# Prefix logsumexp on one core: where the loads stand in ScalarE's instruction stream

## Chip, cores and metric

The kernel runs on one core of a Trainium2 chip. The metric is the device time of one execution in microseconds; lower is better.

## The reference

For each batch and each column the reference runs down the sequence and keeps a running log of a sum of exponentials:

```
B, S, D = 4, 4096, 4128                       # x is random normal, float32
out[:, 0, :] = x[:, 0, :]
for t in range(1, S):
    mx = np.maximum(out[:, t-1, :], x[:, t, :])
    out[:, t, :] = mx + np.log(np.exp(out[:, t-1, :] - mx) + np.exp(x[:, t, :] - mx))
```

So `out[b, t, d]` is the log of the sum of `exp(x[b, s, d])` over all `s` up to `t`. Input and output are 270.5 MB each.

## The kernel before

The kernel computes Exp of the input, prefix sums, and Ln of the sums, and does not keep a running maximum (a last flag sends unsuitable data to a slow general path, `_general`, which is not taken here).

**Tiles.** A tile ("step" in the code) holds 128 x r consecutive rows of one batch and all 4128 columns; partition p holds r neighbouring rows. r is 3 for most tiles and 2 for seven of them. There are n = 45 tiles, numbered 0 to 44: 11 for each of the first three batches (tiles 0, 16 and 27 have two rows) and 12 for the last one, where tiles 37, 39, 43 and 44 have two. A tile lives in one of four slots in SBUF (`SLOTS = 4`, `x0` to `x3`), tile t in slot t mod 4, and everything is done in place: the load writes the slot, Exp, the sums and Ln rewrite it, the store reads it. So load t + 4 may only start once store t has landed; its instruction waits for that.

**Chunks.** The columns are worked on in three chunks (`NC = 3`) of 1376. For each chunk: ScalarE's `exp` (L125); VectorE's `sums` (L153 and L163), which add a partition's own rows; `head`, matmuls on TensorE with a triangular matrix (L171) that give each partition the sum of all rows above it; VectorE's `add`, which adds that to the rows (L187 and L196 for chunks 0 and 1, L181 for chunk 2); and ScalarE's `log` (L206 and L207 for chunks 0 and 1, a pair of Ln; L202, one Ln, for chunk 2). VectorE's `fold` (L143) carries the last sums of a tile into the next one. `head`, `add` and `log` of a chunk need those before them, and the `add` of a tile needs the `fold` that needs the Exp of chunk 2.

**Queues.** All transfers of the main path are issued from ScalarE's queue: `load` (L104; tiles 1 and 2 row by row, L106) and `store` (L111). ScalarE's sequencer takes its instructions in order. A DMA instruction that must wait holds back every Exp and Ln behind it. A store waits for the three Ln of its tile.

**Order.** Three lists, `act`, `vec` and `pe`, fix the order on ScalarE, VectorE and TensorE. They are written by the loop over t near the end of the function: for each chunk c it appends some Exps of the next tile (`exps`, how many is in `turns` or `usual_turn`), then `log`, `add` and `head` of tile t; after the chunks comes `store` t and, in the kernel before, at once the load of tile t + 3 (for t from 2 on), whose slot was emptied by store t - 1. The usual order on ScalarE is: Ln of chunk 0, two Exps of the next tile, Ln of chunk 1, Exp, Ln of chunk 2, store, load. Two places differ: load 4 comes after the second Exp of tile 3, and load 44 (the last) comes right behind load 43 after store 40, though its slot is the one that store 40 empties. The loads of tiles 0 to 3 stand ahead of everything.

Of the kernel before, what the change touches and what calls it, by code (L numbers as in the profile page):

```python
# [15 lines left out]
SLOTS = 4  # L16
# [8 lines left out]
def kernel(  # L25
# [87 lines left out]
    class Chunk:  # L113
# [36 lines left out]
        def sums(self):  # L150
            r, e, got = self.t.r, self.row, []
            if r == 3:
                got.append(nc.vector.tensor_tensor(out=e[1], in0=e[0], in1=e[1], op=ALU.add))  # L153
                for free in () if self.passed else made.get(("log", self.t.n - 1, self.c), ()):
                    tc.add_manual_dep(
                        got[0].ins, free.ins.name,
                        mybir.DependencyInfo(
                            mybir.DependencyClass.Sync, mybir.DependencyReason.DATA,
                        ),
                        reason="the next sum writes what this Ln reads",  # L160
                    )
            n = P if self.passed else P - 1
            got.append(nc.vector.tensor_tensor(  # L163
                out=self.z[0:n], in0=e[r - 2][0:n], in1=e[r - 1][0:n], op=ALU.add,
            ))
            return got
# [46 lines left out]
    steps = []  # L213
# [11 lines left out]
    n = len(steps)  # L225

    lists = {"act": [], "vec": [], "pe": []}
    act, vec, pe = lists["act"], lists["vec"], lists["pe"]
# [17 lines left out]
    }  # L246
    given = {"exp": [0] * n, "sums": [0] * n}

    due = []

    def exps(t, k):
        while t < n and given["exp"][t] < k:
            act.append(("exp", t, given["exp"][t]))
            given["exp"][t] += 1
            if due and given["exp"][t] == due[0][1]:
                act.append(("load", due.pop(0)[0]))

    def passing(t):
        if t and steps[t - 1].last:
# [4 lines left out]
    def sums(t, k):  # L264
        while t < n and given["sums"][t] < k:
# [3 lines left out]
            if c == PASSED - 1 and t:  # L269
                passing(t)  # L270

    exps(0, 2)
    for t in range(n):
        ahead_exps, ahead_sums = turns.get(t, usual_turn)
        exps(t, NC)
        sums(t, 2)
        for c in range(NC):
            exps(t + 1, ahead_exps[c])
            act.append(("log", t, c))
            sums(t + 1, ahead_sums[c])  # L280
            vec.append(("add", t, c))
            if c == 0:
                sums(t, NC)
            pe.append(("head", t, c))
        act.append(("store", t))
        if t == 1:
            due.append((SLOTS, 2))
        elif t and t + SLOTS - 1 < n - 1:
            act.append(("load", t + SLOTS - 1))
            if t + SLOTS == n - 1:  # L290
                act.append(("load", n - 1))
        exps(t + 1, ahead_exps[NC])
        sums(t + 1, ahead_sums[NC])
    passing(n)
# [151 lines left out]
```

## Time and profile before

| | |
|---|---|
| time, median of 3 runs | 1279.49 us (1278.05 to 1281.15) |
| the profiled execution's own time | 1278.78 us |
| its span, first to last instruction | 1277.0 us |
| VectorE busy | 1047.4 us (82%) |
| ScalarE busy | 929.8 us (73%) |
| TensorE matmul busy | 579.5 us (45%) |
| bytes read and written | 270.53 MB and 270.53 MB, 424 GB/s over the span |

Times in the rows of the profile count from the first instruction of the profiled execution. On engines' names: PE is TensorE, PEld its weight loads, DVE VectorE, ACT ScalarE, and ACTq stands for what ScalarE's sequencer issues, the DMAs here. A row of the timeline has the start, the duration, the engine, the line, the operation and the tiles, and in brackets the idle time before it and what ended that. For a DMA row the duration is that of the issuing instruction (with the wait between two that are merged in one row); the time to landing stands in other views. A row for L125 with x2 merges two Exps.

### The profile page before, as it was taken

The numbers are of one execution on the slowest core, as the hardware profiler recorded it, in microseconds if no ns is written. First come the engines' busy times: TensorE is split into PE (matmuls) and PEld (weight loads), VectorE is DVE, ScalarE is ACT, GpSimd is POOL, SyncE is SP. The second block draws the span as 40 slices with busy tenths as digits, with TensorE's granted clock in tenths as the row PEclk, the third lists the DMA queues.
The fourth block names the chain that finished last, engine by engine and source line by source line (L and its number), as shares of the span: only waits on it lengthen the run. The fifth ranks groups of instructions, "written<-read, shape, count | busy, mean of one in ns | idle before, by whom it ended". The sixth has DMA issues, their size and how long they took to land.

```text
span 1277.0 us, 2720 instructions
## 1 busy us (share of the span) xinstructions
PE 579.5 (45%) x812; PEld 225.4 (18%) x812; DVE 1047.4 (82%) x534; ACT 929.8 (73%) x367; POOL 3.8 (0%) x16
## 2 busy tenths in 40 slices
PE   3454544544454353354544424345445435444163
PEld 1121211211111121122111111112112112112021
DVE  3998978888988697798898858689889868788395
ACT  6977877777767676697677668588767767675594
POOL 1000000000000000000000000000000000000000
PEclk9667656665666686666665657676666666776576
DMA  9999999999999999999999999999999999999968
GB/s 398 429 432 432 430 434 434 430 433 434 433 431 432 435 435 431 434 430 422 430 439 430 435 431 436 432 432 427 419 424 444 424 437 434 440 390 424 395 298 364
DMA packets 13550, 541.24 MB, mean 424 GB/s; under 512 B 1504, under 2 KB 1504, under 8 KB 1504
## 3 DMA queue, kind: packets, MB, share of 16 engines
q10 hardware_dynamic: 13536, 541.07, 98.6%
q8 instruction: 6, 0.10, 0.0%
q14 instruction: 8, 0.07, 0.0%
HBM read 270.53 MB, written 270.53 MB: 424 GB/s over the span
## 4 chain that ended last, share of the span: by engine, by line
DMA 49%; ACT 34%; DVE 15%; ACTq 1%; issue 0%
DMA x<-in_x_dram 36%; ACT x L125 21%; DMA out_dram<-x 13%; ACT x L202 5%; ACT x L206 5%; DVE x L187 5%; DVE z L196 3%; ACT x L207 3%; DVE x L181 2%; DVE x L143 2%; DVE x L163 1%; DVE z L163 1%; DVE x L153 1%; ACTq L111 0%; DVE z L190 0%
## 5 line engine op out<-in xcount | busy, mean ns | idle before, releaser
L171 PE MATMUL p<-z,carried 128*128 128x512 f32 (+1 forms) x492 | 356.1, 888 | 472.8 <-DVE z L163 304.2
L125 ACT ACTIVATE x<-x 128x4128 f32<-128x4128 f32 (+1 forms) x135 | 461.5, 3452 | 125.3 <-DMA x<-in_x_dram 89.3
L206 ACT ACTIVATE x<-x 128x2752 f32<-128x2752 f32 (+1 forms) x90 | 208.0, 2312 | 200.6 <-DVE z L196 165.1
L153 DVE TENSOR_TENSOR x<-x 128x1376 f32<-128x1376 f32 x114 | 180.8, 1586 | 180.2 <-ACT x L125 180.2
L171 PEld LDWEIGHTS p<-z,carried 128*128 128x128 f32 x492 | 138.6, 300 | 691.9 <-DVE z L163 336.3
L171 PE MATMUL p<-x,summed 128*128 128x512 f32 (+1 forms) x270 | 189.8, 865 | 151.2 <-DVE x L163 151.2
L187 DVE TENSOR_TENSOR x<-p,x 128x2752 f32<-128x2752 f32 (+1 forms) x90 | 250.9, 2788 | 1.3 <-PE p L171 0.9
L181 DVE SCALAR_TENSOR_TENSOR x<-p,inner,x 128x4128 f32<-128x4128 f32 (+1 forms) x45 | 193.0, 4288 | 1.3 <-PE p L171 1.2
L163 DVE TENSOR_TENSOR z<-x 127x1376 f32<-127x1376 f32 x90 | 143.2, 1591 | 20.6 <-ACT x L125 18.0
L202 ACT ACTIVATE x<-x 128x4128 f32<-128x4128 f32 (+1 forms) x45 | 155.3, 3450 | 4.0 <-DVE x L181 4.0
L196 DVE TENSOR_TENSOR z<-x 128x1376 f32<-128x1376 f32 x82 | 130.6, 1592 | 2.8
L171 PEld LDWEIGHTS p<-x,summed 128*128 128x128 f32 x270 | 73.3, 289 | 264.6 <-DVE x L163 176.8
L207 ACT ACTIVATE x<-z 128x1376 f32<-128x1376 f32 x90 | 120.0, 1333 | 0.0
L163 DVE TENSOR_TENSOR x<-x 128x1376 f32<-128x1376 f32 x45 | 71.6, 1591 | 1.3
L143 DVE TENSOR_TENSOR x<-p,x 1x1376 f32<-1x1376 f32 x41 | 64.7, 1577 | 8.9 <-ACT x L125 8.9
L171 PE MATMUL p<-z,below 128*128 128x512 f32 (+1 forms) x48 | 33.7, 864 | 55.2 <-DVE z L163 42.1
L171 PEld LDWEIGHTS p<-z,below 128*128 128x128 f32 x48 | 13.3, 297 | 76.3 <-issue 32.1
L135 DVE TENSOR_REDUCE short<-x 1x1 f32<-1x4128 f32 x3 | 13.3, 4430 | 0.0
L190 DVE CUSTOM_DVE_ANT_0 z<-x 128x1376 f32<-128x1376 f32 x8 | 12.7, 1592 | 0.3
L146 DVE TENSOR_REDUCE probe<-p 1x1 f32<-1x1376 f32 x4 | 6.3, 1571 | 0.0
L348 ACT ACT_TABLE_LOAD x1 | 1.3, 1283 | 4.8 <-issue 4.8
L128 ACT ACTIVATE x<-x,twice 1x1376 f32<-1x1376 f32 x3 | 4.3, 1441 | 0.2
(23 smaller groups left out, 6.8 us busy)
## 6 DMA issues: line engine op xcount, KB each, us to landing
out_dram<-x ACTq DMA_DIRECT2D x38, 6192.0 KB, 26.0
x<-in_x_dram ACTq DMA_DIRECT2D x36, 6192.0 KB, 40.2
x<-in_x_dram ACTq DMA_DIRECT2D x7, 4128.0 KB, 31.9
out_dram<-x ACTq DMA_DIRECT2D x7, 4128.0 KB, 24.1
x<-in_x_dram ACTq DMA_DIRECT2D x6, 2064.0 KB, 27.7
```

The lines of the kernel that those rows point to most:

```text
L125: got = [nc.scalar.activation(self.e, self.e, ACT.Exp)]
L135: return [nc.vector.tensor_reduce(out=short[:, self.t.b - 1:self.t.b], in_=self.t.xt[0:1, 0, :], op=ALU.min, axis=AX.X,)]
L143: return [nc.vector.tensor_tensor(out=to, in0=pt[0:1], in1=to, op=ALU.add)]
L153: got.append(nc.vector.tensor_tensor(out=e[1], in0=e[0], in1=e[1], op=ALU.add))
L163: got.append(nc.vector.tensor_tensor(out=self.z[0:n], in0=e[r - 2][0:n], in1=e[r - 1][0:n], op=ALU.add,))
L171: nc.tensor.matmul(self.pt[:, a:b], lhsT=w, rhs=self.z[:, a:b], start=True, stop=True,)
L181: return [nc.vector.scalar_tensor_tensor(out=self.e, in0=base, scalar=inner[:, 0:1], in1=self.e, op0=ALU.mult, op1=ALU.add,)]
L187: got = [nc.vector.tensor_tensor(out=e, in0=base, in1=e, op=ALU.add)]
L196: nc.vector.tensor_tensor(out=self.z, in0=ends[0], in1=ends[1], op=ALU.add)
L202: return [nc.scalar.activation(self.e, self.e, ACT.Ln)]
L206: nc.scalar.activation(e, e, ACT.Ln),
L207: nc.scalar.activation(self.row[r - 1], self.z, ACT.Ln),
```

## The change

The change moves `load` instructions within ScalarE's list and nothing else; the other engines' lists stay as they were. `due` becomes a table from tile number to a count of steps, and a new function `turn` appends a step (an `exp` or a `log`; the Ln pair of one chunk counts as one) and then counts down, appending each load whose count has come to zero.

- After the store of a 3-row tile t (t from 2 on) the load of tile t + 3 comes one step later.
- After the store of a 2-row tile it comes two steps later. For t = 1 it is two steps as well; load 4 then stands behind the first Exp of tile 3 instead of the second.
- Load 44 is given six steps from store 40 on. These are Ln of tile 41 chunk 0, two Exps of tile 42, Ln of chunk 1, an Exp, and Ln of chunk 2: the load stands behind that Ln and ahead of store 41.

```diff
-    due = []
+    due = {}
+
+    def turn(step):
+        act.append(step)
+        for t in sorted(due):
+            due[t] -= 1
+            if due[t] == 0:
+                del due[t]
+                act.append(("load", t))
 
     def exps(t, k):
         while t < n and given["exp"][t] < k:
-            act.append(("exp", t, given["exp"][t]))
+            turn(("exp", t, given["exp"][t]))
             given["exp"][t] += 1
-            if due and given["exp"][t] == due[0][1]:
-                act.append(("load", due.pop(0)[0]))
...
             exps(t + 1, ahead_exps[c])
-            act.append(("log", t, c))
+            turn(("log", t, c))
...
         act.append(("store", t))
-        if t == 1:
-            due.append((SLOTS, 2))
-        elif t and t + SLOTS - 1 < n - 1:
-            act.append(("load", t + SLOTS - 1))
-            if t + SLOTS == n - 1:
-                act.append(("load", n - 1))
+        if t and t + SLOTS - 1 < n - 1:
+            due[t + SLOTS - 1] = 1 if steps[t].r == 3 and t > 1 else 2
+        if t + SLOTS == n - 1:
+            due[n - 1] = 6
         exps(t + 1, ahead_exps[NC])
```

## The prediction

> **What bounds the kernel now.** I read first the page's slices, queues and transfer sizes.
>
> ```profile
> GB/s 398 429 432 432 430 434 434 430 433 434 433 431 432 435 435 431 434 430 422 430 439 430 435 431 436 432 432 427 419 424 444 424 437 434 440 390 424 395 298 364
> q10 hardware_dynamic: 13536, 541.07, 98.6%
> out_dram<-x ACTq DMA_DIRECT2D x38, 6192.0 KB, 26.0
> x<-in_x_dram ACTq DMA_DIRECT2D x7, 4128.0 KB, 31.9
> ```
>
> All traffic is on one queue (q10), whose packets fill 98.6% of the 16 DMA engines' span. Most slices run at 429 to 435 GB/s; the last two at 298 and 364. No engine is near that, so the question is where the queue runs empty. Stretches of time show it (columns: stretch, length, busy time and count of PE, PEld, DVE, ACT, POOL, clock, DMA share, GB/s):
>
> ```profile
> 300.00:400.00 100.00, 44.84 (x59) 16.97 (x58) 84.61 (x43) 72.41 (x27) 0.00 (x0) 0.64 1.00 433
> 896.00:902.00 6.00, 3.88 (x5) 1.80 (x6) 5.93 (x4) 2.71 (x2) 0.00 (x0) 0.61 1.06 380
> 1116.00:1124.00 8.00, 4.54 (x7) 1.92 (x8) 7.97 (x7) 6.32 (x4) 0.00 (x0) 0.79 0.81 347
> 1155.00:1207.00 52.00, 13.48 (x20) 5.66 (x21) 28.43 (x15) 28.98 (x11) 0.00 (x0) 0.62 1.00 432
> 1208.00:1220.00 12.00, 6.77 (x10) 2.48 (x8) 11.93 (x7) 9.33 (x4) 0.00 (x0) 0.57 0.55 234
> 1230.00:1240.00 10.00, 6.55 (x11) 2.50 (x9) 9.97 (x6) 9.57 (x5) 0.00 (x0) 0.74 0.55 238
> 1250.00:1255.00 5.00, 3.66 (x6) 1.45 (x6) 4.97 (x5) 2.61 (x2) 0.00 (x0) 0.73 0.86 370
> 1260.00:1268.00 8.00, 0.19 (x2) 0.09 (x2) 4.09 (x6) 4.17 (x3) 0.00 (x0) 0.66 0.71 305
> ```
>
> Against 433 GB/s the four last stretches miss (433 - 234)/433 x 12 = 5.5 us, 4.5, 0.7 and 2.4, together 13.1 us; 1116:1124 misses 1.6. The rest of the run leaves almost nothing to win. Why the queue runs dry at the end is in the waits (engine, line, what was waited for: total us, times, longest) and in the timeline of ScalarE and VectorE:
>
> ```profile
> ACT x L125 <- DMA out_dram<-x: 33.7, 6, 6.9
> ACT x L206 <- DMA out_dram<-x: 23.0, 1, 23.0
> 1171.81 0.34 ACTq L111 DMA_DIRECT2D out_dram<-x  x1
> 1172.19 22.57 ACTq L104 DMA_DIRECT2D x<-in_x_dram  x2
> 1172.82 1.59 DVE L196 TENSOR_TENSOR z<-x 128x1376 f32<-128x1376 f32 x1
> 1194.80 2.50 ACT L206 ACTIVATE x<-x 128x2752 f32<-128x2752 f32 x1 [23.02 <-DMA out_dram<-x]
> 1198.44 7.16 ACT L125 ACTIVATE x<-x 128x4128 f32<-128x4128 f32 x2
> 1216.33 0.35 ACTq L111 DMA_DIRECT2D out_dram<-x  x1
> 1222.61 4.87 ACT L125 ACTIVATE x<-x 128x2752 f32<-128x2752 f32 x2
> 1237.05 0.35 ACTq L111 DMA_DIRECT2D out_dram<-x  x1
> 1252.09 0.34 ACTq L111 DMA_DIRECT2D out_dram<-x  x1
> 1264.61 0.34 ACTq L111 DMA_DIRECT2D out_dram<-x  x1
> ```
>
> Store 40 goes at 1171.81, loads 43 and 44 right behind. Load 44 refills the slot that store 40 empties, so ScalarE's sequencer stands until that store has landed, at 1194.4. The Ln behind it had its input at 1172.82 + 1.59 = 1174.4. The whole tail chain (Ln 41, Exp 42, Ln 41, store 41, then stores 42, 43, 44) starts 20 us late, and no load is left to hide that.
>
> **The change, the last load first.** Landings of load 44 (issued 1194.41), store 41 (1216.33) and all stores (the smallest is the last one's):
>
> ```profile
> DMA to landing us min/median/max: 19.4/19.4/19.4
> DMA to landing us min/median/max: 16.7/16.7/16.7
> DMA to landing us min/median/max: 11.1/26.0/33.7
> ```
>
> A 3-row tile is 6192 x 1024 B = 6.34 MB, 14.6 us at 433 GB/s; a 2-row tile 4128 KB, 9.7 us. Load 44 landed at 1213.8, which is store 40's 1194.4 plus 9.7 (load 43) plus 9.7: the queue works in order, each landing one transfer after the one before. Into an empty queue store 41 took 16.7 - 14.6 = 2.1 us more, so a transfer keeps the queue full if it is issued 2.1 us before its predecessor lands.
>
> Now load 43 stands behind Ln 41 chunk 0, and load 44 behind six steps, the last of them Ln 41 chunk 2, right ahead of store 41. ScalarE goes on at 1174.4, the Ln pair ends at 1178.1, and Exp 42 meets load 42, which lands 14.6 us before store 40, at 1179.8. From the two Exps' start to store 41 the timeline has 1216.33 - 1198.5 = 17.8 us; so store 41 goes at about 1180.0 + 17.8 = 1197.8. Load 44's wait ends at 1194.4, just when its place comes up (3.5 us before store 41, the last Ln's length); queued behind it is only that store, which waits for the Ln anyway. From store to store the timeline has 20.7, 15.0 and 12.5 us: stores 42, 43, 44 go at 1218.5, 1233.6 and 1246.1. The covers for that: Exp 43 starts 6.3 us behind store 41, at 1204.1, as load 43 lands; Exp 44 comes behind store 42, after 1218.5, load 44 landed at 1213.8. Queue: load 44 1213.8, store 41 1228.4, store 42 1243.0, store 43 1252.7, store 44 1262.4. The issues are needed by 1211.7, 1226.3, 1240.9, 1250.6: margins 13.9, 7.8, 7.3 and 4.5 us, so no pause is left. The end moves from 1264.61 + 11.1 = 1275.7 to 1262.4, 13.3 us; by the stretches above it is 13.1. I take 13.2. VectorE's share in the chain is inside the store-to-store distances.
>
> **Loads one step behind the store, 3-row tiles.** A usual place, by the timeline and the chain of waits (start, duration; a DMA's piece is issue to landing):
>
> ```profile
> 410.31 26.02 DMA out_dram<-x
> 412.95 2.50 ACT L206 ACTIVATE x<-x 128x2752 f32<-128x2752 f32 x1 [2.67 <-DVE z L196]
> 415.36 1.33 ACT L207 ACTIVATE x<-z 128x1376 f32<-128x1376 f32 x1
> 293.35 40.20 DMA x<-in_x_dram
> 333.57 7.18 ACT x L125 x2
> ```
>
> The step is a Ln pair that waits 2.67 us for VectorE, so the load goes between 415.4 and 416.7 instead of 410.7, up to 6 us later. The store ahead of it lands at 436.3: the load still has 20 us in the queue, and its landing, fixed by the transfers ahead, doesn't move. Price nothing; without that cover each load would pay its delay. Behind it on ScalarE stands the next Exp or Ln, which loses 0.4 us of issue time as before. Load 4 comes one Exp earlier instead; if it must wait for store 0, it holds the next Exp by one Exp's length at most (7.18 / 2 = 3.6 us), in a slice (the third) that runs at 432 GB/s. Also nothing.
>
> **Two steps behind a 2-row tile's store.** ScalarE stood on an earlier store at six loads (33.7 us), all near 2-row tiles; it now computes at least one step first. Around five of them the slices show 431 to 437 GB/s, so that gives nothing. The sixth is behind the 2-row tile 37 (its store, load 40, store 38; then landings of load 40 and store 38):
>
> ```profile
> 1082.25 0.34 ACTq L111 DMA_DIRECT2D out_dram<-x  x1
> 1088.70 0.35 ACTq L104 DMA_DIRECT2D x<-in_x_dram  x1
> 1120.56 0.34 ACTq L111 DMA_DIRECT2D out_dram<-x  x1
> DMA to landing us min/median/max: 34.0/34.0/34.0
> DMA to landing us min/median/max: 17.0/17.0/17.0
> ```
>
> Load 40 stood 6.1 us on store 36; the two Exps now ahead of it fill that, and store 38 moves from 1120.6 to about 1114, before its need at 1088.7 + 34.0 - 2.1 = 1120.6. Load 40 landed at 1122.7, store 38 at 1137.6, 14.9 against 14.6: by landings the pause cost 0.2 to 0.3, by the stretch's GB/s up to 1.6. I take 0.2, as the end is a landing. The longest delay is where two Ln pairs stand ahead of the load:
>
> ```profile
> 490.08 24.28 DMA out_dram<-x
> 503.96 1.33 ACT L207 ACTIVATE x<-z 128x1376 f32<-128x1376 f32 x1
> ```
>
> Load 19 then goes at about 505 instead of 490.5; the store ahead lands at 514.4, so 9 us are left. Also free.
>
> **A rule against the change.** The row says that a load 6 us later lands at the same time, since 26 us of transfers stand ahead of it. The Trainium skill, "DMA: Bandwidth & Descriptors", section "Rules for kernel authors", advises the opposite of this edit: issue a DMA early, compute, and wait late, which hides its fixed cost. What that would make of the time is the third rival.
>
> **Sum.** 13.2 + 0.2 = 13.4 us. The profiled execution took 1278.78 us (span 1277.0, 1.8 around it), the runs' median is 1279.49: 1265.4 against the first, 1266.1 against the median.
>
> **Rivals.** *A shallow queue is served slower* (slower). In 896:902 the DMAs were busy (1.06) and moved 380 GB/s: 0.7 us lost without a pause, inside load 32, which was issued at 868 and landed 35.4 us later:
>
> ```profile
> DMA to landing us min/median/max: 35.4/35.4/35.4
> ```
>
> It had 35.4 - 14.6 = 20.8 us of transfers ahead of it, instead of the usual 40.2 - 14.6 = 25.6. After the change some 40 loads have 20 or less. If each lost 0.7, that is 28 us: 1294. It decides from 0.34 us a load. Against it: 1155:1207 ran at 432 though load 44, with 19.4 - 9.7 = 9.7 us ahead of it, came later still. 7 in 100.
> *The tail is bound by its chain.* If Exp, Ln and VectorE run slower side by side with the DMA, or a wait I left out comes in, the 4.5 us margin of store 44 goes first; a chain 10 us late costs 5.5 us, 1272. 8 in 100.
> *The load's issue sets the cycle.* The chain of waits runs through loads: 293.35 + 40.2 ends where Exp begins. If a load landed 6 us later for 6 us later issue, one load in two tiles on the chain, 20 such links give 120 us: 1386. The in-order landings speak against it: 2 in 100. This is the time that follows from the rule of the Trainium skill named above.
> *Nothing moves*, because load 44's wait ends no earlier and store 41 stays behind it: 1279; 3 in 100, as the margin after store 40's landing is 17 us.
>
> **Numbers.** The forecast has 80 in 100. Below it: the rest of the 1.6 us pause, and slow stretches like 896:902 that may fall elsewhere (0.7 us each, some four or five in a run), to 1261. Above: the tail's case, 1272. A measurement tells about 0.2%, 2.6 us, from no change. Faster 0.88, same 0.03, slower 0.09.
>
> **What would show it.** Right: the stretch of the last 70 us at 433 GB/s to the last store; store 41 near 1198 and store 44 near 1246, both landing far behind their issue; the 23.0 us wait gone; usual loads about 35 us from issue to landing instead of 40. Wrong: pauses between the last stores, GB/s under 430 in the middle, or Exp waiting longer for loads.

## The result and the profile after

The changed kernel takes 1260.28 us (median of 5, 1259.47 to 1261.07), the kernel before 1279.49 us (median of 5, not of 3 as the table ahead has it; 1278.05 to 1281.15). The ratio is 0.9849, 95% interval 0.9835 to 0.9864: 19.2 us less, where 13.4 were forecast. The direction was right, the size was not: 1260.28 lies 0.7 us below the range's lower end of 1261. The profiled execution took 1260.26 us, span 1258.5. Of the runs below, one of the ten with loads 21 and 32 moved was in a slow state, 1393.01 us, and stands in no ratio.

The page of the kernel after, GB/s in the 40 slices and the share of the queue:

```profile
GB/s 398 425 439 433 429 431 430 433 435 435 427 436 438 425 440 430 437 429 431 441 435 430 432 430 433 431 437 435 435 433 428 435 432 435 433 431 436 427 437 357
q10 hardware_dynamic: 13536, 541.07, 99.6%
```

Only the first slice and the last, in which the queue starts and ends, are low; the queue's share rose from 98.6 to 99.6%. Stretches of the kernel after (columns as before; the last is GB/s):

```profile
300.00:400.00 100.00, 46.24 (x61) 17.93 (x60) 84.98 (x43) 72.42 (x27) 0.00 (x0) 0.64 1.00 434
896.00:902.00 6.00, 3.16 (x5) 1.00 (x3) 3.36 (x2) 1.55 (x1) 0.00 (x0) 0.78 0.99 429
1108.00:1118.00 10.00, 7.20 (x12) 2.89 (x12) 9.60 (x7) 6.30 (x4) 0.00 (x0) 0.72 0.97 421
1188.00:1250.00 62.00, 29.25 (x50) 11.53 (x50) 51.61 (x34) 44.75 (x23) 0.00 (x0) 0.73 1.00 434
```

The tail, 1188 to 1250, runs without a pause. So does the place of the pause at 1116:1124, here 1108:1118, and 896:902 is no slow stretch any more (429 instead of 380 GB/s). ScalarE's waits and its queue in the tail of the kernel after, and the landings of its stores:

```profile
ACT x L125 <- DMA out_dram<-x: 9.5, 5, 2.6
1166.98 0.35 ACTq L104 DMA_DIRECT2D x<-in_x_dram  x1
1189.08 0.35 ACTq L104 DMA_DIRECT2D x<-in_x_dram  x1
1192.32 0.35 ACTq L111 DMA_DIRECT2D out_dram<-x  x1
1213.29 0.35 ACTq L111 DMA_DIRECT2D out_dram<-x  x1
1228.33 0.34 ACTq L111 DMA_DIRECT2D out_dram<-x  x1
1241.36 0.34 ACTq L111 DMA_DIRECT2D out_dram<-x  x1
DMA to landing us min/median/max: 15.9/26.0/35.5
```

The 23.0 us wait is gone, and the 33.7 us on earlier stores are 9.5. Loads 43 and 44 go at 1167.0 and 1189.1, stores 41 to 44 at 1192.3, 1213.3, 1228.3 and 1241.4. No store lands sooner than 15.9 us after its issue, where the last one before took 11.1 in an empty queue: each now stands behind other transfers.

### The profile page after: what moved, and what is told of

The parts are those of the page before. It is cut to its first block, busy times and chain, and to the rows that moved or that the text cites. A ratio compares the mean times of both kernels' runs of the same rounds, so it can differ in the third digit from the quotient of the medians.

```text
span 1258.5 us, 2720 instructions
## 1 busy us (share of the span) xinstructions
PE 584.9 (46%) x812; PEld 226.6 (18%) x812; DVE 1048.2 (83%) x534; ACT 931.6 (74%) x367; POOL 3.8 (0%) x16
## 3 DMA queue, kind: packets, MB, share of 16 engines
q10 hardware_dynamic: 13536, 541.07, 99.6%
## 4 chain that ended last, share of the span: by engine, by line
DMA 63%; DVE 18%; ACT 16%; PE 1%; issue 0%; ACTq 0%; DVEq 0%
DMA x<-in_x_dram 52%; ACT x L125 11%; DMA out_dram<-x 10%; DVE x L181 4%; DVE x L187 4%; DVE x L153 3%; DVE z L163 3%; ACT x L202 2%; DVE z L196 2%; DVE x L143 2%; ACT x L206 2%; ACT x L207 1%; PE p L171 1%; DVE x L163 0%; DVE z L190 0%
## 5 line engine op out<-in xcount | busy, mean ns | idle before, releaser
L171 PE MATMUL p<-x,summed 128*128 128x512 f32 (+1 forms) x270 | 195.9, 890 | 146.0 <-DVE x L163 146.0
L171 PEld LDWEIGHTS p<-z,below 128*128 128x128 f32 x48 | 13.6, 300 | 75.0 <-issue 32.4
```

Source lines behind the costliest of these rows:

```text
L171: nc.tensor.matmul(self.pt[:, a:b], lhsT=w, rhs=self.z[:, a:b], start=True, stop=True,)
```

## The experiments

The theory was the prediction's: pauses of the queue are what can be won, and a store is early enough if it is issued 2.1 us before the transfer ahead of it lands. Then 5.8 us are unexplained. Rivals: the last load is worth more than 13.2; the pause ahead of store 38 is worth more than 0.2; the slow stretches belong to the order of the program and went with it; or the loads' later place brings something everywhere.

**The last load alone.**

```diff
+        if t == 1:
+            due[SLOTS] = 3
+        elif t and t + SLOTS - 1 < n - 1:
+            act.append(("load", t + SLOTS - 1))
         if t + SLOTS == n - 1:
             due[n - 1] = 6
```

(The edits are against the kernel after; these lines take the place of its `due[t + SLOTS - 1] = ...`, and with them all loads but 44 stand where they stood before.)

> The kernel before with one edit: load 44 six steps behind store 40, ahead of store 41; all other loads right behind their stores. The change gave 19.2 us where 13.4 were forecast. If the forecast sized the last load rightly (13.2 us, the pauses between the last stores), this takes 1279.5 - 13.2 = 1266.3 us and the extra comes from the other loads. If the last load is worth all of it, 1260.3. In both cases the pauses at 1208 to 1268 are gone and stores 41 to 44 go some 18 us earlier.

Measured: 1265.47 us against 1280.19 on the same chip, ratio 0.9879 (0.9864 to 0.9894), 13.6 to 17.4 us. Its profiled execution took 1266.12. The tail of this kernel in the timeline and the stretches:

```profile
1194.94 0.35 ACTq L104 DMA_DIRECT2D x<-in_x_dram  x1
1198.22 0.35 ACTq L111 DMA_DIRECT2D out_dram<-x  x1
1219.11 0.35 ACTq L111 DMA_DIRECT2D out_dram<-x  x1
1234.15 0.34 ACTq L111 DMA_DIRECT2D out_dram<-x  x1
1247.17 0.34 ACTq L111 DMA_DIRECT2D out_dram<-x  x1
1188.00:1255.00 67.00, 33.10 (x56) 12.90 (x54) 57.48 (x36) 50.65 (x25) 0.00 (x0) 0.73 1.00 432
```

The prediction had the stores at 1197.8, 1218.5, 1233.6 and 1246.1. From load 44's landing to store 44's it is 48.8 us here (1214.4 to 1263.1) and was 61.9 before (1213.8 to 1275.7): 13.1 us. By the landings, then, the last load was sized rightly. The interval of the runs begins at 13.6, 0.4 us above what was forecast for it; where that would come from is not shown.

**Load 40 alone**, two steps behind store 37; loads 43 and 44 back to back as before.

```diff
+        elif t == 37:
+            due[t + SLOTS - 1] = 2
```

> The kernel before with one edit: load 40 two steps behind the store of the 2-row tile 37. The forecast gave the pause ahead of store 38 0.2 us: 1279.3. Rival: landings from load 40 to load 42 are 57.0 us apart before and 53.6 after the change (1122.7 to 1179.8, 1120.8 to 1174.4), so the pause and the slow stretches behind it cost 3.4 us: 1276.1. If those slow stretches have nothing to do with the pause, they stay, and the gain is that of the pause alone, 0.2 to 1.6.

Measured: 1276.34 us, ratio 0.9969 (0.9957 to 0.9981), 2.4 to 5.5 us less; the rival with 3.4 was right. Stretches behind the pause, before and then with load 40 moved:

```profile
1132.00:1140.00 8.00, 3.74 (x5) 1.70 (x6) 6.37 (x4) 8.00 (x4) 0.00 (x0) 0.52 1.02 396
1148.00:1154.00 6.00, 4.54 (x6) 1.83 (x6) 5.89 (x4) 2.05 (x3) 0.00 (x0) 0.55 0.91 319
```

```profile
1114.00:1124.00 10.00, 5.66 (x12) 2.25 (x10) 9.61 (x6) 6.29 (x6) 0.00 (x0) 0.84 0.98 426
1132.00:1140.00 8.00, 4.78 (x11) 1.93 (x9) 7.62 (x5) 4.29 (x2) 0.00 (x0) 0.93 1.00 433
1146.00:1154.00 8.00, 1.53 (x4) 0.45 (x2) 6.16 (x3) 5.35 (x3) 0.00 (x0) 0.71 0.95 409
```

Nothing was edited at 1132 and 1148. Store 38 now goes at 1114.4, 8.7 us ahead of load 40's landing, and the slow stretches some 15 and 30 us later, with a DMA share of 1.02 and 0.91, are gone or weaker. They belonged to the late store 38. From load 40's landing to load 42's it is 53.6 us instead of 57.0.

**All steps without the last load's** (`due[n - 1] = 1`).

> The change without its last part: all loads one or two steps behind the store as in the change, but load 44 right behind load 43 (one step behind store 40). Forecast: 0.2 us for these steps, 1279.3. By the result less the forecast's tail: 19.2 - 13.2 = 6.0 us, 1273.5; of it 3.4 at load 40 and the rest in slow stretches such as 582:587 and 896:902, which should then be gone from this profile. If a shallow queue were served slower: over 1279.5.

Measured: 1270.25 us, ratio 0.9918 (0.9904 to 0.9931), 8.8 to 12.3 us less. More than 6.0, because the two parts overlap: with everything before it earlier, store 41 went at 1207.1, 1.1 us ahead of load 44's landing at 1208.2, so its pause cost 1.0 us and not 4.6. With 3.6 from that and 3.0 at load 40 (54.0 us from its landing to load 42's, 57.0 before), some 3 us are left; loads 21 and 32 landed 14.6 us behind their predecessors, without a slow stretch.

**The kernel before again**, for a second profile.

> The kernel before, unchanged, for a second profile. If the slow stretches with a full queue (582:587, 896:902, 1134:1140, 1148:1154, some 1 us each) belong to the program's order, they stand at the same places within 2 us and sum up the same; if they are the memory's or the chip's own, they fall elsewhere, and their sum changes by a us or more.

Its profiled execution took 1278.96 us. Extra time of a landing over one transfer (14.6 us): load 21 had 0.9 and again 1.0, load 32 1.5 and 1.2, load 41 2.8 and 2.7. In the other kernels that keep these stores it is 0.9 to 1.4 at load 21, 0.9 to 1.7 at load 32 and 2.7 to 3.1 at load 41: these stretches belong to the program. Not every extra does: of these two profiles the first alone has store 24 1.4 us late, and the second alone loads 7, 9 and 10, by 0.5 to 0.7 us.

**Loads 20 and 31 alone**, one step behind stores 17 and 28; then **loads 21 and 32 alone**, one step behind stores 18 and 29.

```diff
+        elif t in (17, 28):            # the other kernel: (18, 29)
+            due[t + SLOTS - 1] = 1
```

> The kernel before with loads 20 and 31 one step behind stores 17 and 28, nothing else. ScalarE then doesn't stand 4.4 us on an earlier store, and stores 18 and 29 go some 3.5 us earlier (553.2 to 549.7 and 867.7 to about 862); loads 21 and 32 stay right behind them. Theory 'late store': the slow stretches of loads 21 and 32 (landings 0.9 to 1.5 us late each) come from a store that is issued just as the first DMA engines run out; they go, and the time falls by some 2.2 us. Rival 'store and load issued together': they stay, and the time stays.

> The kernel before with loads 21 and 32 one step behind stores 18 and 29, nothing else; the stores stay where they are. Theory 'late store': the slow stretches stay, no gain. Rival 'store and load issued together': they go, some 2.2 us faster.

Measured: 1277.52 against 1279.62, ratio 0.9984 (0.9974 to 0.9993), and 1280.38, ratio 1.0003 (0.9992 to 1.0013), ten runs each. The first gains about 2 us, the second nothing. The stretches around the end of loads 21 and 32, before, then with loads 20 and 31 moved, then with 21 and 32 moved:

```profile
582.00:589.00 7.00, 4.08 (x6) 1.70 (x6) 6.12 (x3) 2.82 (x3) 0.00 (x0) 0.76 0.99 375
895.00:902.00 7.00, 3.88 (x5) 1.80 (x6) 6.93 (x4) 3.71 (x2) 0.00 (x0) 0.67 1.09 403
```

```profile
582.00:589.00 7.00, 4.23 (x6) 1.71 (x6) 5.16 (x3) 2.03 (x3) 0.00 (x0) 0.76 0.98 425
895.00:902.00 7.00, 4.95 (x6) 1.85 (x6) 4.56 (x3) 2.02 (x2) 0.00 (x0) 0.64 1.05 453
```

```profile
582.00:589.00 7.00, 3.93 (x6) 1.37 (x6) 6.93 (x4) 3.14 (x2) 0.00 (x0) 0.74 0.93 347
895.00:902.00 7.00, 4.27 (x8) 1.43 (x6) 6.93 (x5) 3.74 (x2) 0.00 (x0) 0.74 1.01 368
```

With loads 21 and 32 left right behind their stores but the stores 3 to 5 us earlier, the stretches go; with the loads moved and the stores left, they stay. So it is the late store that makes the load behind it slow, not the load's own place. (The first kernel's profiled execution, 1279.02 us, was the slowest of its ten: store 44 went 1.4 us later behind store 43's landing than before, in the tail's pauses, which this kernel keeps.)

**Stores 18 and 29 made late again in the changed kernel**: each moved behind the Ln pair that follows it.

> The changed kernel with stores 18 and 29 one step later (behind the Ln pair of the next tile's chunk 0), some 5.6 us; their loads stay one step behind them. For the last DMA engine both stores are still in time, so by the forecast's way nothing is lost: 1260.3. Theory 'late store': the slow stretches of loads 21 and 32 come back, 1 to 2.8 us each: 1262.3 to 1265.9.

Measured: 1262.05 us (1259.58 to 1262.8, four runs), ratio 0.9867 (0.9851 to 0.9884). The stores moved 2.8 and 2.4 us, not 5.6 (their loads went 5 us later with them, which cost nothing at the 18 loads of the next experiment). Loads 21 and 32 got 0.5 and 0.8 us of extra time back, against 0.0 in the changed kernel. The time doesn't show it: the interval overlaps with that of the changed kernel, and the profiled execution was the fastest of the four. The landings point the way of the theory, at the size of the smaller delay.

All this by lead, from the landing that the trace gives for each single DMA. Lead is from the store's issue to the landing of the transfer ahead of it; the extra is that of the load behind it over 14.6 us. The last column counts slow packets. A DMA engine moves a 3-row tile in packets of 49,536 bytes, the share of one partition, and such a packet takes 1.83 us as a rule (the median of the trace); counted are those over 2.0 us from the store's issue to the landing of the load.

| store, kernel | lead, us | load behind it, extra us | slow packets |
|---|---|---|---|
| 38, before | 2.2 | 2.8 | 45 |
| 18 and 29, before | 5.0, 5.0 | 0.9, 1.5 | 22, 28 |
| 18 and 29, loads 21 and 32 moved | 5.0, 5.0 | 1.2, 1.7 | 28, 28 |
| 18 and 29, made late | 5.6, 5.6 | 0.5, 0.8 | 12, 12 |
| 15, 26 and 36, before | 7.1, 7.0, 7.1 | 0.0, 0.0, 0.0 | 6, 8, 0 |
| 18 and 29, loads 20 and 31 moved | 8.5, 8.5 | 0.0, 0.0 | 0, 0 |
| 1, before | 4.9 | 0.9 | 10 |
| 1, all steps without the last load's | 4.2 | 0.0 | 8 |
| 1, changed kernel | 3.9 | 0.4 | 4 |

Store 1 doesn't fit: it is late in every kernel and costs little, so lead alone doesn't set the price. The packets also tell these losses from others of the same size: loads 25 and 36 landed 0.9 and 1.0 us late in the changed kernel, with no late store ahead of them and one slow packet each, so there a single engine was late.

**Eighteen loads four steps behind the store** (8 to 15, 22 to 26, 33 to 37), in the changed kernel.

```diff
+            usual_place = 4 < t < 13 or 19 <= t < 24 or 30 <= t < 35
+            due[t + SLOTS - 1] = 4 if usual_place else 1 if steps[t].r == 3 and t > 1 else 2
```

> The changed kernel with 18 of its loads (8 to 15, 22 to 26, 33 to 37) four steps behind the store instead of one; each then has some 3 us of transfers ahead of it for the last DMA engine, and for the first ones nothing. If only the last engine counts (the forecast's way, a landing one transfer after the one before): 1260.3, nothing lost. If a transfer that is issued as the first engines run out costs about 1 us: 18 us more, 1278. The prediction's rival of the shallow queue, 0.7 us a load: 1273.

Measured: 1260.03 us (1259.34 to 1260.68), ratio 0.9849 (0.9833 to 0.9866): nothing lost. But the loads had more lead than was expected. The timeline of ScalarE at one of them, and the speed around it:

```profile
246.00 3.64 ACT L125 ACTIVATE x<-x 128x4128 f32<-128x4128 f32 x1 [5.01 <-DMA x<-in_x_dram]
246.01 0.35 ACTq L104 DMA_DIRECT2D x<-in_x_dram  x1
249.55 3.63 ACT L125 ACTIVATE x<-x 128x4128 f32<-128x4128 f32 x1
255.47 1.33 ACT L207 ACTIVATE x<-z 128x1376 f32<-128x1376 f32 x1
260.00:360.00 100.00, 47.56 (x63) 18.69 (x64) 89.15 (x46) 72.42 (x28) 0.00 (x0) 0.66 1.01 435
```

The load stands behind both Exps and the Ln pair that ends at 256.8, and was issued at 246.0, when the first of them began. It landed 29.2 us later: 14.6 us of lead, not 3. So this doesn't test a queue in which the first engines run out at a load. It does test the shallow queue: 18 loads with 11.1 to 14.7 us ahead of them instead of 18.8 to 24.3, at 435 GB/s. That rival is out.

**Four loads alone** (20, 31, 40 and 44), and **the change again** beside it.

> The kernel before with four loads moved and no other: 20 and 31 one step behind their stores, 40 two steps, 44 six. By the runs so far these are worth 2.1, 3.9 and 13 to 15 us one by one. If they are the whole of the change, this takes as long as the changed kernel, about 1260.3 us (1259.5 to 1261.1), and the other 37 moved loads are worth nothing. If the general step behind the store brings something of its own, this is slower than the changed kernel by over 1 us.

> The changed kernel, unchanged, on the same chip as the four-load kernel, to compare the two: 1260.3 us, and a profile whose only losses of over 0.5 us are the first microseconds, load 3, and single landings such as those of loads 25 and 36.

Measured: 1260.41 (1259.35 to 1261.45) and 1260.03 (1259.14 to 1260.55) against 1279.52; ratios 0.9853 (0.9839 to 0.9866) and 0.9847 (0.9833 to 0.9860). Four moved loads are the whole change; the others bring nothing that can be measured, and no version was faster than the changed kernel.

## Why the prediction was wrong in size

- **The last load, 13.2 us: right by the landings.** 13.1 with this load alone, stores within 1.1 us of the issues worked out; the runs' interval begins at 13.6.
- **Usual loads, nothing: right**, by the four loads alone. The place was off: the load was put between 415.4 and 416.7. In the kernel after it goes with the start of the Ln pair, not behind it, so that usual loads take some 38 us to their landing and not 35 (the last row, from issue to landing):

```profile
412.95 2.50 ACT L206 ACTIVATE x<-x 128x2752 f32<-128x2752 f32 x1 [2.67 <-DVE z L196]
412.95 0.35 ACTq L104 DMA_DIRECT2D x<-in_x_dram  x1
295.99 37.90 DMA x<-in_x_dram
```

- **"I take 0.2" for load 40: the step that failed.** It was read off store 38's own landing, 0.2 to 0.3 late, though the 1.6 of the stretch stood beside it. By the landings the rest of the price fell on the loads behind it, 2.8 us on load 41 and 0.5 on load 42: 3.4 in all, 3.9 by the ratio (2.4 to 5.5). By the packets the pause was 25.4 us of idle time on the engines, 1.6 for each of the 16, and the 45 slow packets of store 38 and load 41, at 1134 to 1152, took 31.5 us more than usual, 2.0 for each. The slow stretches at 1132 and 1148 are these packets; the prediction did not count them.
- **"The queue was full at five of them, so that gives nothing": failed at two.** ScalarE's stand at loads 20 and 31 made stores 18 and 29 late, 5.0 us ahead of the landing before them. By the rule used (2.1 us is enough) that was in time; it cost some 2.4 us at loads 21 and 32.
- **The rule behind both**, that a lead of 2.1 us keeps the queue full, was read off a landing, which is that of the last of the 16 DMA engines, but the engines don't run side by side. Each ends its share of a transfer with a packet of 4 bytes (16 for each of the 94 transfers of the kernel before); by these the engines ended load 20, and began store 18, between 554.3 and 557.9. All 16 moved data until 1118.5; at 1119.0 there were 11, at 1120.0, before store 38 was issued, 7, and at 1121.0 only 2. But engines that run out are not the whole of it: in the profile of before six stood empty at store 29, 2.0 us together, and none at store 18.
- **Sum.** 13.1 (last load) + 3.4 (load 40) + 2.4 (loads 21 and 32) = 18.9, against 19.2 by the medians and 18.5 between the two profiled executions.
- **Rivals.** The shallow queue read a real loss, 896:902, but put it down to load 32's lead; it was store 29's. The chain of the tail, the cycle set by the load's issue, and with it the outcome worked out beside the rule of the Trainium skill ("DMA: Bandwidth & Descriptors", "Rules for kernel authors") did not come: with 18 loads issued some 8 to 12 us later still, the time was the same. That rule speaks of a transfer's fixed cost; the 6 us for each load were worked out from this kernel's rows.

What stays open is why packets are slow as a late store ends and again, on all 16 engines, as the load behind it ends, 14 to 33 us after the store's issue, even where no engine had stood empty. Load 3 ends with 16 slow packets in the kernels before and after, with no late store ahead of it. The runs show that it happens and when, not how.

## What to carry to other kernels

When one queue of DMAs bounds a kernel, look for each place where the issuing engine stands on a DMA, and ask how far ahead of the queue's end the next transfer is issued: here stores 7 us ahead cost nothing, those 5 us ahead 0.9 to 1.7 us (but for store 1), the one 2 us ahead 3 to 4 us, and at least half of that price lay in slow stretches behind the place, without a pause to see. Put what must wait for a landing behind work that can run meanwhile, above all at the last load, after which nothing hides the chain. Price a pause by the landings of the two or three transfers that follow it, not of the first alone.

## What was not expected of the hardware

- The 16 DMA engines end one transfer some us apart (554.3 to 557.9 at load 20, and up to 5.1 us at load 36 in the kernel after), so some can run out before the transfer has landed, as at 1119.0 (load 40 landed at 1122.7).
- A transfer can pay for a late predecessor: with a DMA share of 0.93 to 1.09, 347 to 403 GB/s at the end of loads 21 and 32 instead of 425 and more.
- A DMA instruction is issued well ahead of the Exp and Ln that stand before it, at 246.0 behind work that ended at 256.8; counting steps does not give its time.
